# A channel shuffle whose second load is moved from SyncE to ScalarE

## The chip, the cores and the metric

The kernel runs on one core of a Trainium2 chip. The metric is the device time of one execution in microseconds (us). The time of a version is the median of several runs. Apart from them, one execution is recorded by the hardware profiler; all durations of single instructions and transfers come from it.

## The reference

The input is an fp32 tensor of 16 x 64 x 64 positions with 256 channels each. The channels are 8 groups of 32, and they are interleaved: the channel at (group, place in the group) goes to (place, group). Nothing is computed; 67.1 MB are read and 67.1 MB are written in another order of channels.

```python
x = x.reshape(batch, h, w, groups, channels_per_group)
x = x.transpose(0, 1, 2, 4, 3)
x = x.reshape(batch, h, w, c)
```

## The kernel before

The tensor is treated as 65,536 rows of 256 channels, 1 KB each. They are cut into 16 tiles, given by `_SIZES`: a tile of size q holds 128 x q rows, q of them, next to each other in memory, on every partition. The sizes are 4, 8, 16, twelve times 38, and 28. A tile of size q is therefore q KB on a partition: the first three tiles are 512, 1024 and 2048 KB in all, the large ones 4864 KB (38,912 bytes on a partition), the last 3584 KB. In this document load t, copy t and store t are the three steps of tile t, counted from 0, so load 1 is the second load.

One pass of the loop over `_SIZES` (from L45) writes down three instructions for one tile:

- the load, a DMA from DRAM into `in_tile` (L47), issued by SyncE, whose DMA queue the profile calls q1;
- the copy, one VectorE instruction (L49) that reads `in_tile` with the axes exchanged and writes `out_tile`;
- the store, a DMA from `out_tile` to DRAM (L53), issued by ScalarE, whose DMA queue the profile calls q10.

No work is given to TensorE, and GpSimd only sets four constants before the start. ScalarE does no arithmetic; it issues DMAs.

There are three buffers for `in_tile` and two for `out_tile`, each as large as the largest tile. This sets the order. Load t goes into the buffer of tile t - 3, so SyncE waits for copy t - 3 before it issues load t. Copy t waits for load t to land, and for store t - 2 to land, since it writes that store's buffer. Store t waits for copy t. The order is the program's: `tc.manual_schedule` leaves every engine's instructions in the order in which the loop writes them, and an engine that waits holds all that is written behind. So SyncE's program is the loads 0 to 15, VectorE's the copies 0 to 15 and ScalarE's the stores 0 to 15. Loads 0, 1 and 2 find empty buffers and wait for nothing.

## Time and profile before

| what | value |
|---|---|
| median of 3 runs | 316.71 us (316.44 to 317.62) |
| the profiled execution: its time | 316.46 us |
| the profiled execution: its span | 314.7 us |
| bytes read and written | 67.11 MB and 67.11 MB, 427 GB/s over the span |
| VectorE busy | 119.2 us, 38% of the span, 16 copies |
| a copy of size 4, 8, 16, 38, 28 | 1.08, 2.02, 3.90, 8.80, 6.54 us |
| VectorE waiting for stores to land | 175.9 us, 14 times |
| VectorE waiting for loads to land | 5.5 us, twice |

The span runs from the first to the last instruction, and the time of the same execution also holds what lies around it. In the DMA rows of the profile, the busy share is the mean of the core's 16 DMA engines; a slice is one fortieth of the span, 7.9 us. A DMA instruction has two times: the issue, in which the engine that issues it is occupied, and the landing, when its last byte has arrived and those that wait for it are released. "x us to landing" counts from the start of the issue.

### The profile page before, as it was taken

Reading aid. Unit: us, or ns where it says so; the run is one execution under the profiler, and the core shown is the slowest. Engines: PE = TensorE matmul, PEld = TensorE weight load, DVE = VectorE, ACT = ScalarE, POOL = GpSimd, SP = SyncE. Lnnn points to the kernel's source line nnn. Section 1 sums busy time; section 2 is a strip of 40 time slices with the busy share of each in tenths; the row PEclk is TensorE's granted clock in tenths of the full one; section 3 lists DMA queues with packets and bytes.
Section 4 is the critical chain, followed back from the end, with each engine's and each line's share of the span. In section 5 each row is a group of like instructions: output and inputs, shape, how many; then the busy total and the mean of one; then the engine's idle time right before and its main releaser. Section 6 shows DMA issues by size and latency. Waiting matters only on the chain.

```text
span 314.7 us, 133 instructions
## 1 busy us (share of the span) xinstructions
DVE 119.2 (38%) x16; POOL 0.2 (0%) x4
## 2 busy tenths in 40 slices
DVE  3040645505506407407308209109109019046620
POOL 0000000000000000000000000000000000000000
DMA  8999999999999999999999999999999999999997
GB/s 308 452 398 454 413 419 466 396 475 396 455 415 445 425 430 440 425 445 415 455 396 470 401 465 406 460 411 460 411 460 411 460 411 455 428 395 454 455 418 306
DMA packets 4608, 134.22 MB, mean 427 GB/s; under 512 B 512, under 2 KB 512, under 8 KB 768
## 3 DMA queue, kind: packets, MB, share of 16 engines
q1 hardware_dynamic: 2304, 67.11, 49.8%
q10 hardware_dynamic: 2304, 67.11, 49.4%
HBM read 67.11 MB, written 67.11 MB: 427 GB/s over the span
## 4 chain that ended last, share of the span: by engine, by line
DMA 75%; DVE 20%; issue 0%; SPq 0%; DVEq 0%
DMA out_dram<-out_tile 74%; DVE out_tile L49 20%; DMA in_tile<-in_x_dram 2%; SPq L47 0%; DVEq L49 0%
## 5 line engine op out<-in xcount | busy, mean ns | idle before, releaser
L49 DVE COPY out_tile<-in_tile 128x9728 f32<-128x9728 f32 (+4 forms) x16 | 119.2, 7449 | 181.4 <-DMA out_dram<-out_tile 175.9
L71 POOL MEMSET const-bfloat16-1.0<- 128x1 bf16 x1 | 0.1, 102 | 0.0
L71 POOL MEMSET const-uint8-127<- 128x1 uint8 x1 | 0.1, 102 | 0.0
L71 POOL MEMSET const-float32-1.0<- 128x1 f32 x1 | 0.1, 99 | 0.0
L71 POOL MEMSET const-float32-0.0<- 128x1 f32 x1 | 0.1, 98 | 0.2 <-issue 0.2
## 6 DMA issues: line engine op xcount, KB each, us to landing
in_tile<-in_x_dram SPq DMA_DIRECT2D x12, 4864.0 KB, 46.8
out_dram<-out_tile ACTq DMA_DIRECT2D x12, 4864.0 KB, 37.0
in_tile<-in_x_dram SPq DMA_DIRECT2D x1, 3584.0 KB, 43.8
out_dram<-out_tile ACTq DMA_DIRECT2D x1, 3584.0 KB, 13.3
in_tile<-in_x_dram SPq DMA_DIRECT2D x1, 2048.0 KB, 11.0
out_dram<-out_tile ACTq DMA_DIRECT2D x1, 2048.0 KB, 26.7
in_tile<-in_x_dram SPq DMA_DIRECT2D x1, 1024.0 KB, 5.4
out_dram<-out_tile ACTq DMA_DIRECT2D x1, 1024.0 KB, 25.8
```

Source lines behind the costliest of these rows:

```text
L49: nc.vector.tensor_copy(out=out_tile[:, : q * c].rearrange("p (i j g) -> p i j g", j=CPG, g=G), in_=in_tile[:, : q * c].rearrange("p (i g ...
L71: nc = _bacc.Bacc("TRN2", target_bir_lowering=False, num_devices=1)
```

## The change

The loop counts its passes, and the load of the second pass, t = 1 (8 KB on a partition, 1024 KB in all), is issued by ScalarE and no longer by SyncE. All other loads stay on SyncE. The sizes, buffers, copies and stores are as before. The load stands in the program where it stood, as the first of the three instructions of its pass. The lines below it are one further down in the changed kernel: the load is L48 there, the copy L50, the store L54.

```diff
-    for q in _SIZES:
+    for t, q in enumerate(_SIZES):
         in_tile = in_pool.tile([P, biggest * c], F32, name="in_tile")
-        nc.sync.dma_start(out=in_tile[:, : q * c], in_=rows(x_flat, first, q))
+        queue = nc.scalar if t == 1 else nc.sync
+        queue.dma_start(out=in_tile[:, : q * c], in_=rows(x_flat, first, q))
         out_tile = out_pool.tile([P, biggest * c], F32, name="out_tile")
         nc.vector.tensor_copy(
```

The programs of the engines after it are: SyncE loads 0, 2, 3 and so on to 15; ScalarE store 0, load 1, store 1, store 2 and so on to 15; VectorE unchanged.

## The prediction

> **What bounds the kernel now.** I read the page's DMA rows first, then the stretches of the span, then the early timeline with the landings. In the page the 16 DMA engines are busy from the second slice to the last but one:

> ```profile
> DMA  8999999999999999999999999999999999999997
> ...
> DMA packets 4608, 134.22 MB, mean 427 GB/s; under 512 B 512, under 2 KB 512, under 8 KB 768
> q1 hardware_dynamic: 2304, 67.11, 49.8%
> q10 hardware_dynamic: 2304, 67.11, 49.4%
> ```

> VectorE is busy only 38% of the span. q1 holds the loads, q10 the stores; together they fill 99.2%. The stretches (us, VectorE, GpSimd, clock, DMA share, GB/s) show where that begins and ends:

> ```profile
> 0.00:1.70 1.70, 0.00 (x0) 0.20 (x4) 1.00 0.00 0
> 1.70:2.00 0.30, 0.00 (x0) 0.00 (x0) 1.00 1.13 205
> ...
> 2.00:4.00 2.00, 0.00 (x0) 0.00 (x0) 1.00 1.01 383
> ...
> 12.00:300.00 288.00, 115.52 (x14) 0.00 (x0) 1.00 1.00 433
> 300.00:312.00 12.00, 0.55 (x1) 0.00 (x0) 1.00 1.02 442
> ```

> Nothing moves before 1.70 us, then the engines never pause until the last store. So the order of the DMAs is free, and any pause of all 16 engines adds its whole length to the time. VectorE's 175.9 us of waiting for stores is only this full machine seen from another side.

> Packets give the second fact. 32 DMAs of 128 partitions make 4096; the other 512 are small ones, 16 a DMA. So one partition's row is one packet, 8 rows an engine for every DMA, whatever its size. At 433 / 16 = 27.1 GB/s an engine takes 0.15 us for a 4 KB row, 0.30 for 8 KB, 0.61 for 16 KB and 1.44 for the 38,912 bytes of a large tile. The DMA view of 12.5 to 18 us, when large load 3 meets small store 0, shows how they share:

> ```profile
> DMA packets 96, 2.06 MB, mean 375 GB/s; under 512 B 0, under 2 KB 0, under 8 KB 48
> q1 hardware_dynamic: 48, 1.87, 78.5%
> q10 hardware_dynamic: 48, 0.20, 8.7%
> ```

> 48 rows from each queue: the queues take turns by row, not by byte. This is why 512 KB of store 0 needs 15.1 us to land. The start, from the timeline and the DMA issues:

> ```profile
> 0.73 23.88 SPq L47 DMA_DIRECT2D in_tile<-in_x_dram  x6
> 4.09 1.08 DVE L49 COPY out_tile<-in_tile 128x1024 f32<-128x1024 f32 x1 [4.09 <-DMA in_tile<-in_x_dram]
> 5.20 19.45 ACTq L53 DMA_DIRECT2D out_dram<-out_tile  x3
> 6.59 2.02 DVE L49 COPY out_tile<-in_tile 128x2048 f32<-128x2048 f32 x1 [1.42 <-DMA in_tile<-in_x_dram]
> 20.36 3.90 DVE L49 COPY out_tile<-in_tile 128x4096 f32<-128x4096 f32 x1 [11.75 <-DMA out_dram<-out_tile]
> ```
> ```profile
> in_tile<-in_x_dram SPq DMA_DIRECT2D x1, 1024.0 KB, 5.4
> out_dram<-out_tile ACTq DMA_DIRECT2D x1, 1024.0 KB, 25.8
> in_tile<-in_x_dram SPq DMA_DIRECT2D x1, 512.0 KB, 3.3
> out_dram<-out_tile ACTq DMA_DIRECT2D x1, 512.0 KB, 15.1
> ```

> Load 1 (1024 KB) lands at 6.56 us, copy 1 ends at 8.6, and load 4, which reuses load 1's buffer, is issued then, long before load 3 is through.

> [...] an issue takes 0.37 us here, and q1 alone takes 100.4% of the engines from 5.2 to 9.3 us. [...] ScalarE's first issue is held to 5.20 us, by copy 0.

> **The change part by part.** *Off SyncE:* one issue of about 0.4 us, so load 2 goes at 1.1 to 1.2 us instead of 1.6. Worth nothing: load 0's rows cover it to 3.4 us. *Onto ScalarE:* its program is store 0, load 1, store 1 and so on, since a loop pass writes its store after its load and load 1 belongs to the second pass. Load 1 has no wait of its own, but store 0 waits for copy 0, until 5.2 us. Load 1 is issued at about 5.6 us, 4.4 us later than now, and stands on q10 behind store 0's eight rows.

> What that does: SyncE issues load 3 at 5.2 us as before (its buffer is freed by copy 0), then stops at load 4, which needs copy 1. q1 holds the rest of load 2 and 8 rows of load 3; q10 holds 8 rows of store 0, then 8 of load 1. Turn by turn q1's rows, fewer and already ahead, finish first, and load 1 comes last. Until it has landed and been copied there is nothing else: loads 4 and 5 wait on SyncE behind copy 1, store 1 on ScalarE for the same copy, and copy 2 on VectorE behind copy 1 though its data is long there.

> The work before that point is 8 rows each of loads 0, 1, 2, 3 and store 0: 8 x (0.15 + 0.30 + 0.61 + 1.44 + 0.15) = 21.2 us an engine. It starts at 1.7; the slow first rows lose 0.4 us (the two stretches from 1.70 to 4.00 moved 0.83 MB, which is 1.9 us of 433 GB/s, in 2.3 us). So the engines run dry at 23.3 to 23.6 us.

> The pause then: landing of the last row, copy 1 of 2.02 us, dispatch under 0.1, and the way from an issue to the first row. Landing and first row together are what load 0 takes over its data: 3.3 - 1.2 = 2.1 us. Sum 2.1 + 2.0 + 0.1 = 4.2. In that 2.1 is the 0.4 of slow first rows; if a restart in mid-kernel has none, 3.8; if the landing is 0.3 to 0.4 shorter too, since the last rows of 16 engines differ by some tenths, 3.4. I take **3.8**, with 3.4 and 4.2 as bounds.

> After it (about 27 us) load 4 and store 1 start together, load 5 and store 2 follow copy 2 at about 31. The next thing needed is copy 3, which needs store 1: 8 x (1.44 + 0.30) = 14 us, so 41 to 42, copy 8.8, load 6 on its way at about 52. Loads 4 and 5 and stores 1 and 2 are 8 x (2 x 1.44 + 0.30 + 0.61) = 30 us of rows, to 57. Covered by 4 to 5 us. From there two large loads and two large stores are always queued. Loads will run some rows further ahead, so the last part has stores alone for longer; there a large store is 8 x 1.44 = 11.5 us, and the other buffer's copy with landing, dispatch and first row is 8.8 + 1.6 = 10.4. Covered, by 1.1 us only. So both cost nothing.

> Sum on the profiled execution: its time was 316.46 (span 314.7, the rest around it). 316.46 + 3.8 = **320.3 us**. The median of the runs is 316.71, 0.25 above it; the middle would be 320.5 from there, inside the range.

> **The rivals.**

> *Same: load 3 covers the detour.* If load 1 lands before load 3 is 3 us from its end (copy and first row), load 4 arrives in time. It decides at about 18 us of landing. If the queues shared by bytes, 1.57 MB of store 0 and load 1 at half of 433 GB/s would take 7.3 us from about 6.2, load 1 landing near 14. Then no pause, and 316.5, with 316.2 to 317.5. Also here: that the change does what its words say, load 1 issued at 0.7 us; then load 0 and load 1 merely share and load 2 covers, 316.5 again. Against the first stands 48 against 48 rows; against the second ScalarE's program order.

> *Slower by more: one queue runs ahead at the restart.* Store 0 was issued at 5.20, but q10 moves nothing before 9.3 us: rows that the other queue had waiting go first, about five of load 2, as if they were taken up in advance. If load 4 gets such a lead over store 1, five rows of 1.44 us delay store 1 by 7 us, copy 3 and load 6 with it, and the cover of 4 to 5 us is gone: a second pause of about 1 us, or up to 1.4 with a late restart. That gives 321.3 to 322. For it: the lead is seen. Against it: load 4 and store 1 are released by the same copy and dispatched within 0.1 us, so neither finds rows of the other waiting.

> *Faster* has almost nothing to take from: only the 1.7 us before the first row, which load 0 alone sets.

> **How the numbers follow.** A measurement here can tell about 0.5%, or 1.6 us, from no change. One pause (319.9 to 320.7, with run scatter 319.6 to 321.0): 0.78. A second pause as well: 0.13. Same: 0.07. Faster: 0.02. So slower 0.91, same 0.07, faster 0.02. The range takes the first case with its scatter and most of the second: 319.4 to 321.8.

> **What would show it.** Right: in the profile after, ScalarE's issues begin with store 0 at about 5.2 us and load 1 right after; load 1 takes 17 to 19 us to land; copies 1 and 2 stand back to back from about 24 us; the DMA row has a dent in the slice at 23.6 to 31.5 us, and a stretch of 3.4 to 4.2 us at no GB/s; later slices as before. Wrong: load 1 landing by 18 us, or no dent; or a second dent near 57 us, which is the last rival.

## The result and the profile after

The changed kernel takes 331.72 us (median; 330.92 to 331.79) against 316.71: 1.046 times as long, with a 95% interval of 1.044 to 1.048. The prediction said 320.3 and a range up to 321.8. The direction is right, the size is four times too small. The profiled execution took 331.79 us (span 330.0), 15.3 more than that of the kernel before. Here and below, a ratio and its interval leave out executions more than 1.5% above the fastest one of the same kernel.

The page's DMA rows of the changed kernel:

```profile
DMA  8987999999999999999999999999999999999996
GB/s 318 412 383 258 457 413 429 409 406 424 410 420 377 453 377 443 387 443 387 424 406 420 410 401 429 401 429 377 453 377 443 387 439 427 393 464 434 401 455 292
DMA packets 4608, 134.22 MB, mean 407 GB/s; under 512 B 512, under 2 KB 512, under 8 KB 768
q10 hardware_dynamic: 2448, 68.16, 50.9%
q1 hardware_dynamic: 2160, 66.06, 47.0%
```

The dent that was forecast is there, 258 GB/s in the fourth slice. But the mean is 407 GB/s where it was 427, and the slices after the dent stay busy and yet move less. The timeline shows the forecast start, line by line (start, duration, engine, line; in brackets the idle time before):

```profile
5.25 0.38 ACTq L54 DMA_DIRECT2D out_dram<-out_tile  x1
5.66 0.50 ACTq L48 DMA_DIRECT2D in_tile<-in_x_dram  x1
24.74 5.79 DVE L50 COPY out_tile<-in_tile 128x2048 f32<-128x2048 f32 x2 [19.52 <-DMA in_tile<-in_x_dram]
43.58 8.98 DVE L50 COPY out_tile<-in_tile 128x9728 f32<-128x9728 f32 x1 [13.06 <-issue]
```

Load 1, whose buffer was free from the start, is issued behind store 0 at 5.66 us: ScalarE held it while store 0, written ahead of it, waited for copy 0 until 5.25 (in load1_first below, where it is written ahead of store 0, it goes at 0.72). VectorE has nothing to do for 19.5 us, and copies 1 and 2 stand back to back from 24.74. The stretches (columns as before) put a size on the pause:

```profile
24.40:27.70 3.30, 2.96 (x2) 0.00 (x0) 1.00 0.00 0
27.70:30.00 2.30, 2.30 (x1) 0.00 (x0) 1.00 1.00 271
30.00:69.00 39.00, 18.33 (x3) 0.00 (x0) 1.00 1.02 432
69.00:275.00 206.00, 70.91 (x8) 0.00 (x0) 1.00 1.00 412
```

Nothing moves for 3.3 us, and after it 2.3 us run at 271 GB/s, which loses (1 - 271/433) x 2.3 = 0.9. The stretch from 24.0 to 24.4 was already down to 41 GB/s, another 0.4. Together 4.6 us. From 30 to 69 us the rate is 432 GB/s, the old one. Then it falls to 412 and stays there to 275 us, at full busy share: 206 x (1 - 412/433) = 10 us that the prediction has no term for. Pause and slow stretch make 14.6 of the 15.3 us. In the kernel before, the same stretch:

```profile
69.00:275.00 206.00, 79.37 (x9) 0.00 (x0) 1.00 1.01 435
```

Which rows became slow is in the DMA view of 100 to 250 us (packets, MB, share of 16 engines' time), first of the kernel before, then of the changed one:

```profile
q10 hardware_dynamic: 934, 32.61, 50.3%
q1 hardware_dynamic: 941, 32.26, 49.7%
```
```profile
q10 hardware_dynamic: 883, 30.62, 52.1%
q1 hardware_dynamic: 896, 31.13, 48.0%
```

The large rows are 0.038912 MB, and 16 engines have 2400 us in this window. A store row (q10; load 1 has long gone) took 0.503 x 2400 / (32.61 / 0.038912) = 1.44 us before and 0.521 x 2400 / (30.62 / 0.038912) = 1.59 us after. A load row took 1.44 us in both. Added up over the packet records of the whole trace, the large store rows cost each engine 10.1 us more.

A packet record gives queue, start, duration and bytes of one row, but names neither the DMA engine nor the partition. Both are inferred here and below. A row in the middle of the kernel starts within 10 ns of the end of another one, and rows chained in this way make 16 sequences with eight rows of every DMA of 128 partitions in each; a sequence is taken for an engine. The j-th row of a load and the j-th row of a store on one engine are taken for the same partition.

One more view, the DMA issues with the median time to landing, shows what else is different in this stretch; first before, then after:

```profile
in_tile<-in_x_dram SPq DMA_DIRECT2D x12, 4864.0 KB, 46.8
out_dram<-out_tile ACTq DMA_DIRECT2D x12, 4864.0 KB, 37.0
```
```profile
in_tile<-in_x_dram SPq DMA_DIRECT2D x12, 4864.0 KB, 39.1
out_dram<-out_tile ACTq DMA_DIRECT2D x12, 4864.0 KB, 39.3
```

Load t+3 and store t are issued in the same moment, when copy t ends (about 0.03 us behind it, in both kernels). Before, the load landed 9.8 us after the store. After the change they land together: they go through their eight rows an engine side by side. I call the difference, divided by the time of one load row and one store row, the **lag** of the loads: 9.8 / 2.88 = 3.4 rows before, 0 after. The experiments ask whether the lag, and not the pause or ScalarE, makes store rows slow.

### The profile page after: what moved, and what is told of

The parts are those of the page before. It is cut to its first block, busy times and chain, and to the rows that moved or that the text cites. A ratio compares the mean times of both kernels' runs of the same rounds, so it can differ in the third digit from the quotient of the medians.

```text
span 330.0 us, 133 instructions
## 1 busy us (share of the span) xinstructions
DVE 119.9 (36%) x16; POOL 0.2 (0%) x4
## 2 busy tenths in 40 slices
DMA packets 4608, 134.22 MB, mean 407 GB/s; under 512 B 512, under 2 KB 512, under 8 KB 768
## 3 DMA queue, kind: packets, MB, share of 16 engines
HBM read 67.11 MB, written 67.11 MB: 407 GB/s over the span
## 4 chain that ended last, share of the span: by engine, by line
DMA 72%; DVE 19%; issue 4%; ACTq 0%; DVEq 0%
DMA out_dram<-out_tile 65%; DVE out_tile L50 19%; DMA in_tile<-in_x_dram 7%; ACTq L54 0%; DVEq L50 0%
## 5 line engine op out<-in xcount | busy, mean ns | idle before, releaser
L50 DVE COPY out_tile<-in_tile 128x9728 f32<-128x9728 f32 (+4 forms) x16 | 119.9, 7499 | 196.1 <-DMA out_dram<-out_tile 159.4
## 6 DMA issues: line engine op xcount, KB each, us to landing
in_tile<-in_x_dram ACTq DMA_DIRECT2D x1, 1024.0 KB, 19.1
out_dram<-out_tile ACTq DMA_DIRECT2D x1, 1024.0 KB, 16.7
```

The source lines that it names most:

```text
L50: nc.vector.tensor_copy(out=out_tile[:, : q * c].rearrange("p (i j g) -> p i j g", j=CPG, g=G), in_=in_tile[:, : q * c].rearrange("p (i g ...
```

## The experiments

The theories that the expectations name. **Pause:** only the pause costs. **Level** (also called alignment): a store row is slow when it is next to the load row of the same partition. **Lockstep:** store rows are slow when all engines are in the same turn. **Lead:** they are slow with the largest lead of loads over stores. **Addresses:** they are slow at certain distances of the DRAM addresses. The edits are shown shortened to the lines that matter. The halves, store_moved, same_source, level_two, one_off and early_off are built on load1_first; late_on_sync and the kernels whose names begin with before are built on the kernel before, those that begin with after on the changed kernel.

### Load 1 on ScalarE, but ahead of store 0 (load1_first)

```diff
+    load(0)
+    load(1)          # nc.scalar, written before the loop
     for t, q in enumerate(_SIZES):
+        if t > 1:
+            load(t)
```

> Load 1 on ScalarE, but written ahead of store 0, so that it is issued at 0.7 us. No pause at 24 us by any theory. Pause theory (only the pause and what follows from it costs): 316.5 to 317. Alignment theory (a store row is slow when it directly follows the load row of the same partition, that is when load t+3 and store t run through their rows side by side): by the row-by-row working, loads t+3 and stores t land together here too, so the store rows take about 1.58 us and the time is about 326. Lockstep theory (store rows are slow when all 16 engines are in the same turn, whatever rows they are at): slow or fast as the phases of the engines fall, between 316.5 and 326, and store rows of 1.58 us only where the starts of one row on 16 engines lie within 0.6 us.

Measured: 325.68 us, ratio 1.028 (1.026 to 1.029). There is no pause; the DMA row has a 9 in every slice between the first and the last. Issues and the view of 100 to 250 us:

```profile
in_tile<-in_x_dram SPq DMA_DIRECT2D x12, 4864.0 KB, 38.8
out_dram<-out_tile ACTq DMA_DIRECT2D x12, 4864.0 KB, 39.0
```
```profile
q10 hardware_dynamic: 912, 31.13, 52.6%
q1 hardware_dynamic: 905, 30.86, 47.6%
```

Lag 0, store rows 1.58 us. So slow store rows come without a pause, and cost about 9 us by themselves; the pause theory falls. The 326 of the level theory was worked out from the turns before the run.

### Small loads that shift the turns (after_shift4, after_half1, before_shift5)

Each adds one load of 512-byte rows into a scratch tile on SyncE, to take turns of q1 and move hardly any bytes:

```diff
+        if t == 7:   # before_shift5: t == 5
+            nc.sync.dma_start(out=extra[:n, :], in_=x_flat[: n * 128].rearrange("(p f) -> p f", p=n))
         in_tile = in_pool.tile([P, biggest * c], F32, name="in_tile")
```

with n = 64 and n = 8 in the changed kernel, n = 80 in the kernel before.

> The changed kernel with one more small load (64 rows of 512 bytes into a scratch tile) before load 7 on SyncE: four turns of q1 on each of the 16 engines, so that loads fall four rows behind the stores from store 4 on. The pause at 24 us stays. Alignment theory: store rows return to 1.44 us after it, some 9 us come back, 322 to 323. Lockstep theory and any theory that puts the slow rows on the number of tiles between load and store: all engines still move together, nothing returns, 331 to 332.

325.07 us, 1.026 (1.024 to 1.027): 6.7 us came back, not 9. The lag is 3.9 and the store rows are 1.44 us. By the packet records the store rows did give back the 9 us an engine; 1.4 us more than in the changed kernel went to large load rows, in the passage from one lag to the other, and 0.6 to idle time.

> The changed kernel with a small load of 8 rows of 512 bytes before load 7 on SyncE: one more turn of q1 on 8 engines and none on the other 8. Lockstep theory: the two halves are now in opposite turns, all store rows return to 1.44 us, 322 to 323. Alignment theory: the 8 engines without the extra turn stay aligned and slow, the other 8 may recover by one row; the slow half sets the landings, 329 to 332.

336.09 us, 1.060 (1.058 to 1.063), slower than the changed kernel. The packet records, put in order engine by engine, are clearer than the time: after 120 us half of the engines have the store row directly behind the load row of the same partition and take 1.56 to 1.62 us, while nearly all of the other half, shifted by two rows, take 1.44 to 1.45. The view of 100 to 250 us has the mixture, 1.53 us a store row:

```profile
q10 hardware_dynamic: 913, 31.48, 51.6%
```

Idle time an engine is 9.9 us, against 4.0 in the changed kernel. This fits a quick half that waits for the other: a DMA leaves 16 landing records in the trace, taken here for one an engine, and in the changed kernel load 0's come from 3.60 to 4.09 us and copy 0, which waits for it, starts at 4.12, after the last. Lockstep does not fit, since it would have freed all of them.

> The kernel before with a small load of 80 rows of 512 bytes before load 5 on SyncE: five more turns of q1 on every engine, which brings the loads, five rows off, level with the stores (load t+2 beside store t). Alignment theory: store rows rise to about 1.58 us, 316.7 becomes 325 to 327. Lockstep theory: no more than the 0.1 us of the small load unless the engines fall into one phase, 316.5 to 317.5.

317.37 us, 1.001 (0.9995 to 1.003). It missed its aim: the issues show 54.3 us against 37.0, a lag of 6.0 and not 8, so level was not tried. Lag 6 is quick, 1.44 us.

### Splitting by partitions (halves_level, halves_crossed)

```diff
+        for a in (0, 64):    # stores of halves_crossed: (64, 0)
+            queue.dma_start(out=in_tiles[t][a : a + 64, : q * c], in_=rows(x_flat, start, q)[a : a + 64, :])
```

> As load1_first, but every load and every store from tile 3 on is two DMAs of 64 partitions, the lower 64 first in both: control for the next kernel. Every engine still meets a partition's load row and store row one after the other. Alignment theory and lockstep theory: store rows near 1.58 us, 325 to 327. If the splitting itself frees the rows: 317.

> As halves_level, but each store sends its upper 64 partitions first, each load still the lower 64 first: same number of DMAs and turns, all engines in the same turn as in the control, but a store row follows the load row of a partition 64 away. Alignment theory (partition or address): store rows back to 1.44 us, 316.5 to 318. Lockstep theory: as the control, 325 to 327.

Medians of 423 and 417 us over all executions: both useless for the question, since the split itself makes the kernel slow (376 GB/s in halves_level and 366 in halves_crossed from 100 to 250 us, where the kernel before has 432). No run shows why.

### The DRAM addresses (store_moved, same_source)

```diff
+        move = 405 if t > 2 else 0          # store_moved: in the store's address
+        if q == biggest: start = P * 28     # same_source: in load()
```

> As load1_first, but stores 3 to 15 write 405 KB further on in DRAM, and the last store only 112 of its 128 partitions, so that the output is the reference's in another place and with a gap. On-chip rows and turns as in load1_first. If the slow rows come from the DRAM addresses of a load and a store that run side by side at a fixed distance (14.25 MB for three tiles): back to 1.44 us, 316 to 318. If they come from the partitions on chip, or from lockstep: 325 to 326.

Ratio 1.036 (1.033 to 1.040), lag 0, store rows 1.58 us, with stores 3 to 15 in another place of DRAM.

> As load1_first, but the twelve large loads all read the DRAM rows of tile 3, so that the output is wrong from tile 4 on; turns, buffers and stores are unchanged. If the slow store rows come from the distance of the DRAM addresses that are read and written at one time, that distance now changes with every tile: back to 1.44 us on most tiles, 317 to 320. If they come from the turns or the partitions on chip: 325 to 326.

Ratio 1.031 (1.028 to 1.035), lag 0, store rows 1.58 us on the whole. The distance between the addresses read and written is another for each tile here, and the rows are as slow as before. The address theory falls, as far as these two kernels reach. The packet records again split by engine: from 80 us on, where the store row is directly behind the load row of its partition it takes 1.61 to 1.62 us until 240 us; on three engines that got out of step it takes 1.44, in the same stretches.

### Row shares and the pause (after_quarters)

```diff
+        if t == 3:
+            for a, b in ((0, 10), (10, 20), (20, 29), (29, 38)):
+                queue.dma_start(out=in_tile[:, a * c : b * c], in_=src[:, a * c : b * c])
```

> The changed kernel, with load 3 as four DMAs of about a quarter of the columns each, so that q1 has 32 rows of about 9.5 KB in place of 8 of 38 KB. If queues share by rows, the 16 rows of store 0 and load 1 pass beside 16 of these: load 1 lands at 18 to 19.5 us instead of 24.7, and load 4 is issued at about 21, before load 3 is through, so the pause of 3.4 us and the slow restart of 1 us are gone. Whether the store rows are slow later then depends on how loads and stores fall to each other: 316.5 to 318 if not level, 326 to 327 if level. If sharing goes by bytes or time, load 1 lands as in the changed kernel and nothing is gained.

320.12 us, 1.010 (1.008 to 1.012). The stretches around the place of the pause:

```profile
20.00:24.00 4.00, 4.00 (x2) 0.00 (x0) 1.00 1.02 433
24.00:28.00 4.00, 1.70 (x1) 0.00 (x0) 1.00 1.13 481
```

No pause. Load 1 lands in 14.4 us instead of 19.1 and copy 1 starts at 19.91, with the same bytes in the same queues; only the rows of load 3 are more and shorter. This is the turn by row at work. The lag came to 3.0 and the store rows to 1.44 us. It ends 2 us above the forecast: from 295 to 305 us, where stores run alone, it moves 393 GB/s, so there the copy is no longer hidden; against 433 GB/s that is 0.9 of the 2 us, and the rest stays open.

### Level by another number of tiles, and one row beside (level_two, one_off)

```diff
+        if t == 6:           # level_two, in load(): two column halves
+            for a in (0, q // 2): ...
+        if t == 7: ...       # one_off: a small load, n = 16
```

> As load1_first, but load 6 is two DMAs of half the columns each, which takes eight turns of q1 more: afterwards load t+2 (no longer t+3) runs level with store t, row beside row of the same partition. Level theory (slow rows come from neighbouring turns on one partition): still slow, 325 to 326. Lead theory (they come with the largest lead that the buffers allow, three tiles less nothing): store rows back to 1.44 us from about 85 us on, 317 to 319.

Ratio 1.031 (1.024 to 1.037), store rows 1.57 us. Its issues:

```profile
out_dram<-out_tile ACTq DMA_DIRECT2D x12, 4864.0 KB, 39.2
in_tile<-in_x_dram SPq DMA_DIRECT2D x11, 4864.0 KB, 63.3
```

24.1 us apart: at 1.57 + 1.44 a pair that is a lag of 8.0, so load t+2 runs level with store t. The lead theory falls, level stands.

> As load1_first, with one more load of 16 rows of 512 bytes before load 7: one turn more on every engine, so that the loads are one row short of level. Level theory: a store row now follows the load row of another partition, back to 1.44 us, 317 to 319. Lead theory, with a lead that is only one row smaller: still slow on most rows, 323 to 326.

320.29 us, 1.011 (1.009 to 1.013), over the 319 of the level theory. Landings of 39.9 and 37.0, lag 1.0, store rows 1.44. By the packet records large load rows took 2.0 us an engine more than 1.44 a row would make, of which the kernel before also has 0.4, and store rows 1.1. The store rows lost nearly all of it from 60 to 80 us, the load rows most of theirs from 80 to 120 us.

### ScalarE left out (late_on_sync)

```diff
+        if t == 0:           # behind store 0, all on nc.sync
+            load(3)
+            load(1)
```

> All loads on SyncE as in the kernel before, but load 1 is written behind load 3, so that it comes last of the early DMAs without ScalarE having any part in it. If it is the place of load 1 in the order that costs and not the engine: the same pause of 3.4 us at about 24 us, loads and stores start again together and run level, 331 to 332. If the shared ScalarE queue is the cause: 317 to 320.

330.30 us, 1.043 (1.041 to 1.044). Two of its stretches:

```profile
24.20:27.50 3.30, 2.94 (x2) 0.00 (x0) 1.00 0.00 0
27.50:30.00 2.50, 2.50 (x1) 0.00 (x0) 1.00 0.92 269
```

The same pause of 3.3 us and the same restart as in the changed kernel, then lag 0 and store rows of 1.58 us. ScalarE as an issuer has no part in it; the place of load 1 in the order has.

### Out of level early, and into level in the kernel before (early_off, before_level, before_level2)

Small loads once more: 64 rows before load 6 in load1_first; 80 rows before load 5 and 64 (before_level) or 32 (before_level2) before load 6 in the kernel before.

> As load1_first, with one more load of 64 rows of 512 bytes before load 6, so that loads and stores are some rows apart before the first two large tiles meet. Level theory (the store rows are slow at a lag of 0 or 8 rows, not between): a lag of 1 to 4 rows, store rows of 1.44 us from the start, 316.5 to 318. If load 1 on ScalarE itself does harm by another way: clearly above 318.

The profiled execution took 316.44 us, as quick as the kernel before (316.46), with lag 6.0 (not 1 to 4) and all store rows at 1.44. The runs spread from 316.2 to 320.3, median 319.07, ratio 1.005 (1.003 to 1.008); no trace was taken of one near 320. The large loss of load1_first is gone, with load 1 still on ScalarE. But the median lies above the 318 that the expectation had set, so a small loss in other executions, with a cause of its own, stays possible.

> The kernel before with small loads of 512-byte rows before load 5 (80 rows) and load 6 (64 rows). The first alone brought the lag from 3.4 to 6.0 rows; both should bring it to about 8, where load t+2 runs level with store t. Level theory: if the landings show a lag of 8, store rows near 1.58 us and 323 to 326; if the lag comes out at 7 or 9, 1.44 us and 317 to 318.5. If slow rows need a kernel with load 1 on ScalarE or late: 317 at any lag.

1.002 (1.000 to 1.004): it overshot, lag (60.3 - 31.5) / 2.88 = 10.0, quick, 1.44 us.

> As before_level, with 32 rows in place of 64 before load 6. The 64 rows moved the lag by four, from 6 to 10, past the level; 32 should move it by two, to 8. Level theory: at a lag of 8 store rows near 1.58 us and 323 to 326. If slow rows need load 1 late or on ScalarE: 1.44 us and 317 to 318 at a lag of 8. At another lag than 8 it decides nothing.

Ratio 1.002 (1.001 to 1.004). Its issues and its view of 100 to 250 us:

```profile
in_tile<-in_x_dram SPq DMA_DIRECT2D x12, 4864.0 KB, 59.9
out_dram<-out_tile ACTq DMA_DIRECT2D x12, 4864.0 KB, 36.7
```
```profile
q1 hardware_dynamic: 931, 32.49, 50.1%
q10 hardware_dynamic: 928, 32.38, 49.9%
```

The lag is 23.2 / 2.88 = 8.1, and the store rows take 1.44 us. So the level theory in the form "a lag of 0 or 8 is slow" falls as well. What differs from level_two is the order within a pair, seen in the packet records engine by engine: in level_two, load1_first and the changed kernel the store row comes directly *behind* the load row of its partition, here directly *ahead* of it.

What is left is narrower: **large store rows are slow where the engine has each time just done the large load row of the same partition and goes on with another large load row; outside the short passages from one lag to another and the ends of the kernels, hardly anywhere else.** All kernels together (lag from landings, row time from 100 to 250 us):

| kernel | lag, rows | directly behind the same partition's load row | store row, us |
|---|---|---|---|
| before | 3.4 | no | 1.44 |
| after_quarters, after_shift4 | 3.0, 3.9 | no | 1.44 |
| one_off, before_shift5, early_off, before_level | 1.0, 6.0, 6.0, 10.0 | no | 1.44 |
| before_level2 | 8.1 | no, directly ahead | 1.44 |
| changed kernel | 0 | yes | 1.59 |
| load1_first, store_moved, late_on_sync | 0 | yes | 1.58 |
| same_source | 0 | on most engines | 1.58 (1.61 or 1.44 by engine) |
| after_half1 | 0 | on half of the engines | 1.53 (1.6 or 1.44 by engine) |
| level_two | 8.0 | yes | 1.57 |

The two rows in which engines of one run differ carry most: same time, same kernel, same traffic, and only the engines in that order are slow (1.6 us against 1.44). Why the chip does so stays open. Three things do not fit a simple conflict on a partition.

- *The row behind counts too.* In the changed kernel the last row of store 11 stands directly behind the large load row of its partition and takes 1.44 us; what follows it is the first 28 KB row of load 15. The nine kernels in which this order occurs have 143 such rows, followed by a 28 KB row, a 512-byte row or a store row; 141 of them took less than 1.48 us, although the store rows before them took 1.56 to 1.58 (medians by kernel). Nearly all rows of store 12, between two 28 KB rows of load 15, take 1.44 as well.
- *It sets in over some rows.* The first two rows of the first large store in this order are quick on nearly every engine, in all nine kernels; the fifth is slow on nearly every one. In the changed kernel this is store 3, with medians over the engines of 1.44, 1.44, 1.44, 1.47 and 1.56 us for its first five rows. Of the rows of all later stores in this order, 6235 of 6242 took more than 1.48 us.
- *Small rows are spared.* The rows of stores 1 and 2 take no more than their own normal times beside large load rows of the same partition: in the changed kernel 0.31 and 0.61 us (medians), as in the kernel before.

Apart from these edges, the row behind is always the next row of the loads, so "directly behind load row j" and "directly ahead of load row j + 1" go together in the slow rows of the table. The records can't tell whether only one of the two matters, or both.

A kernel with the same turns and another partition in the store wasn't had, since the split by 64 partitions brings a slowness of its own (366 and 376 GB/s).

## Why the prediction was wrong, point by point

- **Load 1 late, behind store 0: right.** 5.66 us against "about 5.6"; 19.1 us to land against 17 to 19. late_on_sync, with the same pause of 3.3 us and all loads on SyncE, shows that this delay, not the engine, makes the pause.
- **Turn by row: right,** and after_quarters confirms it by taking the pause away with more and shorter rows (load 1 landed in 14.4 us instead of 19.1).
- **The dry point: 23.8 to 24.4 us,** by engine, against 23.3 to 23.6, a little late.
- **The pause: a little small.** 3.3 us of nothing, with its edges 4.6 against 3.8 (3.4 to 4.2). By the packet records an engine stood idle for 3.9 us (median), as forecast. The mis-sized part is the restart: the first large row on each engine took 2.35 us (median), not 1.44. The 3.8 allowed nothing for slow first rows, and the 4.2 only the 0.4 us seen on the small rows of load 0.
- **The cover behind it: right.** Load 6 was issued at 52.6 (about 52 was forecast), and from 30 to 69 us the engines moved 432 GB/s. The second pause of the last rival did not come.
- **"From there two large loads and two large stores are always queued ... So both cost nothing": this step failed.** The engines stayed full, as it says (busy share 1.00). But it carried the row time of 1.44 us over from the kernel before, where the lag is 3.4 rows, while the same paragraph moved the loads "some rows further ahead". Here load 4 and store 1 begin together at the restart and the lag is 0 from then on, and at this lag the store rows took 1.59 us: 10 us. The restart is not needed for it, since load1_first came to lag 0 without one. The same error stands near the start of the prediction: "So the order of the DMAs is free" holds for the bytes, not for the time of a row. Of the 15.3 us only the 4.6 of the pause were in the prediction; that the larger part, which it had at nothing, went in the same direction was luck.
- **"Same" fell for the reason given;** the second form of it (load 1 issued at 0.7 us, 316.5) was tried as load1_first: with load 1 on ScalarE's queue from 0.72 us it took 325.7, 2.8% more than the kernel before. There the pause was judged rightly and the store rows were missed again.

The trace of the kernel before had no slow large store row, so no row of it could price one. It did have the lag in it, 46.8 against 37.0 us, and the forecast that the lag would change; an unknown cost on that side would have belonged in the range.

## What to carry to other kernels

In these kernels two DMA queues shared an engine row by row, so a small DMA that shared with large rows was as late as the large rows made it: load 1 took 19.1 us to land beside 38 KB rows of load 3 and 14.4 us beside rows of about 9.5 KB. So put what others wait for ahead of them in its queue, and look at which instruction stands before it in the issuing engine's program. When transfers bound a kernel, a shift in the start can change the rate long after it, here from 435 to 412 GB/s between 69 and 275 us. So price a new lag between the two queues as unknown and compare GB/s and the time of a row, not the busy share, which was 1.00 at 433 and at 412 GB/s alike.
